# Second feed-forward block of a two-layer trunk: up projection as seven block products, down projection in five chunks

## The chip, the cores and the metric

One core of a Trainium2 chip runs the whole program. The metric is the device time of one execution in microseconds (us). The engines meant below are TensorE (PE, its weight loads shown apart as PEld), VectorE (DVE), ScalarE (ACT), GpSimd (POOL) and SyncE (SP, which here only issues transfers). Each takes its instructions strictly in the order of its own queue.

## The reference

One inference step of a two-layer trunk on 640 tokens of width 1024: 512 tokens of a 64-wide grid and 128 context tokens. Each layer is attention (latent attention in the first, neighbourhood and windowed attention in the second), then a feed-forward block. What the change concerns is the feed-forward block of the second layer:

```
h = modulate(rmsnorm(x), shift, scale)                 # 640 tokens x 1024
u = h @ w_up                                           # 1024 -> 2 * 2816: sides a and g
u = depthwise convolution of 3 taps along the tokens   # zero ends for each group of tokens
x = x + gate * ((u_a * silu(u_g)) @ w_down)            # 2816 -> 1024
y = rmsnorm(x)                                         # behind the second layer
```

All inputs and results are float32.

## The kernel before

Activations lie feature-major: 128 features on the partitions, the tokens along the row. A row has 642 columns: 512 tokens, a zero column, 128 tokens, a zero column; it is processed in two halves, `HALF = ((0, 352), (352, 642))`. A float32 matrix product is made of three passes with float32r operands: each operand is split into a high part (a cast on ACT, line 115) and a low part, the operand less its high part (a subtraction on DVE or POOL, line 111). One product of a 128x128 weight tile with a half of the tokens is so three matmuls: high by high, high by low, low by high (line 135).

The feed-forward block, `ffn_body`, runs over 22 tiles f of 128 inner features, and over two sides for each (a and g). For one f and side, `load_w` brings 512 KB of weights on the SP queue into a tile `raw` of a ring of three, splits them into `whi` and `wlo` (rings of three each), and 48 matmuls go into a two-bank PSUM tile `mm` (8 tiles of 128 input features, 3 passes, 2 halves). `evac` reads that PSUM tile: one ACT activation (middle tap and bias, line 499), two `scalar_tensor_tensor` on DVE (the other taps, lines 500 and 502). When both sides are there: silu on ACT (508), a product on DVE (509), and the split of the result into `g` (cast on ACT, subtraction on DVE).

After 8 tiles f (then 8, then 6) the down projection of these tiles runs over 8 output tiles j, and `add_x` (line 442) adds each result to the residual stream `x` from PSUM. In the last chunk it runs over one half of the tokens and then the other, with the squares for the last norm behind it (line 399 adds them, on POOL or DVE), and a tail that scales and stores the result (line 1525).

In front of the block, `out_proj` makes the attention's output projection half by half; the norm of a half of the tokens (lines 354 to 376, then 419, 432, 433) runs while PE makes the next thing. For the second half PE starts with the first halves of the first three up products (`lead(jobs, h, 3)`): 72 matmuls.

The order of the work in this block is not written out by hand: the program is recorded, and a scheduler lays each engine's queue in order; each instruction then waits, at its place in its queue, for what it needs.

Of the kernel before, what the change touches and what calls it, by code (L numbers as in the profile page):

```python
# [35 lines left out]
HA = 352  # L36
# [6 lines left out]
# The orders in which the steps of a phase are issued; a token names a step, its numbers and, at the end, another engine than Pool  # L43
# for the part of it that may move (d: DVE, a: ACT).
# The steps of mla_in.
# [14 lines left out]
# The units of the attention behind it, two for a head.  # L60
# [6 lines left out]
# The heads of the odd layer, two of a pair after one another.  # L67
# [20 lines left out]
class Trunk:  # L88
# [9 lines left out]
    # ---------------------------------------------------------------- helpers  # L98
# [14 lines left out]
    def split(self, hi, lo, src, lo_engine=None):  # L113
        """Two float32r parts whose sum is src."""
        self.nc.scalar.copy(hi, src)  # L115
        self.low(lo, src, hi, lo_engine)
# [22 lines left out]
    def proj_steps(self, ps, w, rhs, half, stride=P, off=0, m=P, order=None):  # L139
        """Half of the tokens of a feature-major product: (w columns off..off+m of each k tile)^T times rhs."""  # L140
# [14 lines left out]
    def proj_late(self, w, rhs):  # L155
        """A product whose last k tile is left to the function returned."""
# [20 lines left out]
    def acts(self):  # L177
        """A new set of activations [half][k] -> (hi, lo); halves in slots of their own."""
        return [[None] * KT, [None] * KT]

    def act(self, half):
        w = HALF[half][1] - HALF[half][0]
        return tuple(self.T(self.hp, "h" + "ab"[half], [P, w], F32R, 16) for _ in range(2))

    # ----------------------------------------------------- queue of PE filling
# [20 lines left out]
    def after(self, a, b):  # L206
        """Issue a after b, on their common engine."""
# [84 lines left out]
    def mod_step(self, mode):  # L292
        """One k tile of a piece of a modulation vector; mode "d": without the other engines, "i": products in place."""
# [32 lines left out]
    def mod_finish(self, ps_tag, age=0):  # L326
        """The sums over partitions of the vectors whose sums over k tiles were issued a while ago."""
# [1361 lines left out]
```

## Time and profile before

| what | value |
|---|---|
| median of 3 runs | 1730.47 us (1729.17 to 1732.49) |
| profiled execution, first to last instruction (span) | 1726.0 us |
| mean granted TensorE clock | 0.975 |
| PE busy | 1611.3 us, 93% of the span |
| DVE, ACT, POOL busy | 1156.3, 862.9, 594.2 us |

The profile shows one execution; the medians of the runs lie 4.5 us above its span. Rows of groups give line, engine, operation, output tile <- input tiles, shape and count, then total busy time, the mean of one in nanoseconds, and the idle time before. Rows in order of time begin with the start and the length in us; "x3" marks instructions that were merged. Rows of stretches give, after the stretch and its length, the busy time of PE, PEld, DVE, ACT and POOL with their numbers of instructions, the granted clock, the DMA share and GB/s.

### The profile page before, as it was taken

Reading aid. Unit: us, or ns where it says so; the run is one execution under the profiler, and the core shown is the slowest. Engines: PE = TensorE matmul, PEld = TensorE weight load, DVE = VectorE, ACT = ScalarE, POOL = GpSimd, SP = SyncE. Lnnn points to the kernel's source line nnn. Section 1 sums busy time; section 2 is a strip of 40 time slices with the busy share of each in tenths; the row PEclk is TensorE's granted clock in tenths of the full one; section 3 lists DMA queues with packets and bytes.
Section 4 is the critical chain, followed back from the end, with each engine's and each line's share of the span. In section 5 each row is a group of like instructions: output and inputs, shape, how many; then the busy total and the mean of one; then the engine's idle time right before and its main releaser. Section 6 shows DMA issues by size and latency. Waiting matters only on the chain.

```text
span 1726.0 us, 27729 instructions
## 1 busy us (share of the span) xinstructions
PE 1611.3 (93%) x10565; PEld 1542.0 (89%) x10565; DVE 1156.3 (67%) x1901; ACT 862.9 (50%) x1570; POOL 594.2 (34%) x565
## 2 busy tenths in 40 slices
PE   8877888888999999999998999989999999999996
PEld 2777877788899999999998999978999999999996
DVE  4895888768888779977548677763755435543536
ACT  3545767644555345543345678784443213321344
POOL 2164667563253433443063344665100000000044
PEclk9988999989999999999999999998999999999998
DMA  9431221063344444444235111132122222222223
GB/s 337 136 103 51 62 67 63 13 204 104 104 159 142 147 141 154 149 149 131 67 109 174 56 51 52 56 102 89 38 86 74 74 74 75 75 80 77 68 74 116
DMA packets 74850, 176.11 MB, mean 102 GB/s; under 512 B 11134, under 2 KB 22734, under 8 KB 74718
## 3 DMA queue, kind: packets, MB, share of 16 engines
q1 hardware_dynamic: 72222, 170.08, 30.8%
q10 hardware_dynamic: 2304, 4.20, 0.7%
q8 instruction: 83, 1.36, 0.3%
q14 instruction: 49, 0.40, 0.1%
q0 software_dynamic: 192, 0.07, 0.0%
HBM read 167.24 MB, written 8.03 MB: 102 GB/s over the span
## 4 chain that ended last, share of the span: by engine, by line
PE 61%; DVE 11%; ACT 4%; issue 3%; DMA 3%; POOL 1%; DVEq 0%; SPq 0%; ACTq 0%; POOLq 0%
PE mm L135 55%; DMA mraw<-in_w_mod_dram 2%; DVE wlo L111 1%; DVE acc L311 1%; PE sc L1196 1%; PE o L1246 1%; PE tr L1234 1%; DVE nt L419 1%; POOL wlo L111 1%; DVE u L500 1%; ACT whi L115 1%; DVE pt L111 0%; DMA raw<-in_w_out_dram 0%; PE b L354 0%; DVE ha L433 0%
## 5 line engine op out<-in xcount | busy, mean ns | idle before, releaser
L135 PE MATMUL mm<-ha,whi 128*128 128x352 f32 (+1 forms) x1920 | 472.1, 328 | 11.5 <-ACT ha L432 4.6
L135 PE MATMUL mm<-hb,whi 128*128 128x290 f32 (+1 forms) x1920 | 398.3, 300 | 2.6 <-ACT hb L432 1.3
L135 PEld LDWEIGHTS mm<-ha,whi 128*128 128x128 f32 (+1 forms) x1920 | 334.6, 190 | 14.6 <-ACT ha L432 4.7
L115 ACT CAST whi<-raw 128x1024 fp32r<-128x1024 f32 (+2 forms) x194 | 192.9, 999 | 306.6 <-PE mm L135 282.4
L111 POOL TENSOR_TENSOR wlo<-raw,whi 128x768 fp32r<-128x768 f32 (+3 forms) x60 | 125.6, 2099 | 618.9 <-ACT whi L115 551.1
L135 PE MATMUL mm<-g,whi 128*128 128x352 f32 (+1 forms) x1408 | 315.6, 312 | 7.5 <-DVE x L442 7.1
L135 PEld LDWEIGHTS mm<-hb,whi 128*128 128x128 f32 (+1 forms) x1920 | 317.1, 191 | 5.4 <-issue 2.5
L135 PE MATMUL mm<-ha,wlo 128*128 128x352 f32 (+1 forms) x960 | 312.3, 325 | 0.0
L135 PE MATMUL mm<-hb,wlo 128*128 128x290 f32 (+1 forms) x960 | 286.8, 299 | 0.0
L309 POOL TENSOR_TENSOR acc<-acc,mt 128x512 f32<-128x512 f32 x115 | 178.9, 1556 | 258.1 <-ACT mt L308 255.3
L111 DVE TENSOR_TENSOR wlo<-raw,whi 128x1024 fp32r<-128x1024 f32 (+1 forms) x134 | 172.1, 1287 | 117.1 <-ACT whi L115 116.4
L135 PEld LDWEIGHTS mm<-g,whi 128*128 128x128 f32 x1408 | 238.8, 191 | 9.4 <-issue 4.0
L135 PE MATMUL mm<-g,wlo 128*128 128x352 f32 (+1 forms) x704 | 220.2, 313 | 2.4 <-POOL wlo L111 1.6
L311 DVE SCALAR_TENSOR_TENSOR acc<-mraw,cs,acc 128x512 f32<-128x512 f32 (+1 forms) x165 | 163.7, 999 | 49.5 <-DMA mraw<-in_w_mod_dram 47.7
L135 PEld LDWEIGHTS mm<-hb,wlo 128*128 128x128 f32 (+1 forms) x960 | 183.5, 191 | 0.4 <-issue 0.2
L135 PEld LDWEIGHTS mm<-ha,wlo 128*128 128x128 f32 (+1 forms) x960 | 181.6, 189 | 0.5
L442 DVE SCALAR_TENSOR_TENSOR x<-mm,mod,x 128x128 f32<-128x128 f32 (+3 forms) x160 | 71.4, 477 | 129.2 <-PE mm L135 129.2
L308 ACT ACTIVATE mt<-mraw,cs 128x512 f32<-128x512 f32 x115 | 81.8, 720 | 113.3 <-DMA mraw<-in_w_mod_dram 99.0
L135 PEld LDWEIGHTS mm<-g,wlo 128*128 128x128 f32 x704 | 134.0, 190 | 3.4 <-POOL wlo L111 2.2
L500 DVE SCALAR_TENSOR_TENSOR u<-mm,convw,u 128x641 f32<-128x641 f32 x88 | 77.4, 879 | 22.4 <-ACT u L499 22.4
L819 POOL TENSOR_TENSOR p<-p,s 128x640 f32<-128x640 f32 x48 | 63.5, 1343 | 61.2 <-DVE s L812 57.9
L502 DVE SCALAR_TENSOR_TENSOR u<-mm,convw,u 128x641 f32<-128x641 f32 x88 | 77.7, 883 | 2.2
(248 smaller groups left out, 2533.9 us busy)
## 6 DMA issues: line engine op xcount, KB each, us to landing
raw<-in_w_up_dram SPq DMA_DIRECT2D x88, 512.0 KB, 3.4
mraw<-in_w_mod_dram SPq DMA_DIRECT2D x128, 256.0 KB, 2.9
raw<-in_w_down_dram SPq DMA_DIRECT2D x32, 512.0 KB, 3.5
raw<-in_w_down_dram SPq DMA_DIRECT2D x32, 384.0 KB, 3.1
raw<-in_w_in_odd_dram SPq DMA_DIRECT2D x18, 512.0 KB, 3.6
mraw<-in_w_mod_dram SPq DMA_DIRECT2D x16, 512.0 KB, 8.7
raw<-in_w_out_dram SPq DMA_DIRECT2D x16, 512.0 KB, 3.9
x<-in_xT_dram SPq DMA_DIRECT2D x16, 321.0 KB, 6.0
```

Source lines behind the costliest of these rows:

```text
L111: (engine or self.nc.vector).tensor_sub(lo, src, Fv(hi))
L115: self.nc.scalar.copy(hi, src)
L135: self.pe = self.nc.tensor.matmul(out, lhsT=l, rhs=r, start=k == 0, stop=k == n - 1)
L308: nc.scalar.activation(t, raw, AF.Copy, scale=s)
L309: nc.gpsimd.tensor_add(acc, acc, t)
L311: nc.vector.scalar_tensor_tensor(out=acc, in0=raw, scalar=s, in1=acc, op0=ALU.mult, op1=ALU.add)
L419: self.nc.vector.scalar_tensor_tensor(out=t[:, c], in0=x[k][:, c0:c1][:, c], scalar=self.mod[l][:, ma, k, v : v + 1], in1=rs[:, c], op0=AL ...
L442: nc.vector.scalar_tensor_tensor(out=xt[:, a:b], in0=ps[:, a:b], scalar=self.mod[l][:, m, j, v : v + 1], in1=xt[:, a:b], op0=ALU.mult, op1 ...
L500: nc.vector.scalar_tensor_tensor(out=u[:, 1:W], in0=ps[:, 0 : W - 1], scalar=cw[:, j, 0:1], in1=u[:, 1:W], op0=ALU.mult, op1=ALU.add)
L502: nc.vector.scalar_tensor_tensor(out=u[:, 0 : W - 1], in0=ps[:, 1:W], scalar=cw[:, j, 2:3], in1=u[:, 0 : W - 1], op0=ALU.mult, op1=ALU.add)
L819: nc.gpsimd.tensor_tensor(out=p_, in0=p_, in1=u.s[:, j : j + 1].to_broadcast(list(p_.shape)), op=ALU.mult)
L1196: nc.tensor.matmul(ps[:, c : c + n], lhsT=u.Q[:, a], rhs=x[e], start=e == 0, stop=e == 1)
```

## The change

The two halves of the tokens are made equal, 322 and 320 columns, in the whole program (`HA = 322`). For the second layer's feed-forward block a class `Mix` takes the place of `ffn`.

For one f the product has two sides of the output, two halves of the 1024 input features and two halves of the tokens: eight block products of 12 matmuls. With the weight blocks A11, A12 (side a, lower and upper input features) and A21, A22 (side g), and the activation blocks B11, B12, B21, B22 (input features by half of the tokens), they are replaced by seven products (Strassen's identity in Winograd's form): A11 B11, A12 B21, and five products of sums of blocks (T1 to T4 and B22 name their right-hand operands). `norm` makes the sums of the activation blocks once, behind the norm of the second half of the tokens. `mixed` makes four sums of weight blocks for every f, on POOL (lines 1643 to 1647 of the changed kernel), and splits the results: `sp` (1024 wide, low part on DVE), `gp` (1024 wide, in `whi`/`wlo`, low part on POOL) and `s4p` (512 wide, low part on POOL). `up` combines the seven results with two ACT copies (L1628, L1633) and five DVE additions (L1659, L1666, L1667, L1669, L1672), each of a PSUM and an SBUF operand, into two SBUF tiles `u`; `conv` then works on these instead of on PSUM (L1683 to L1689). The first three f begin ahead with A11 B11 and A12 B21 (`LEAD`). The down projection runs in five chunks of 5, 5, 4, 4 and 4 tiles f, each after the up projection of one tile more, and now into one-bank PSUM tiles by half of the tokens. The ring `raw` keeps its three tiles, and now holds both sides' weights of an f until `mixed` is done with them.

```diff
-HA = 352
+HA = 322
...
@@ run
-            with self.psums(wide), self.pool("ffn1") as pool:
...
-                x, h = self.out_proj(pool, 1, oT, xd, lambda: None)
...
+                    x, _ = self.out_proj(pool, 1, oT, xd, lambda: None, mix=mix)
...
-                self.ffn(pool, 1, h, x, lambda n: None, tail)
...
+                    mix.ffn(pool, pi, x, lambda: None, tail)
+class Mix:
...
+    LEAD = 3
+    CHUNKS = ((0, 5), (5, 10), (10, 14), (14, 18), (18, 22))
+    PSUMS = {"p": (1, 6), "b": (1, 2)}
...
+    def norm(self, pool, wpool, x, acc, half):
...
+        for q in range(n):
+            a, b = self.first.pop(q), self.pair()
...
+            for j in range(2):
+                self.shifted(b[:, j], x, rs, 1, q + j * n)
...
+            nc.vector.tensor_sub(a[:, 0], b[:, 0], a[:, 0])
+            nc.gpsimd.tensor_sub(c, b[:, 1], b[:, 0])
+            nc.vector.tensor_sub(b[:, 0], b[:, 1], a[:, 0])
+            nc.vector.tensor_sub(a[:, 1], a[:, 1], b[:, 0])
+            self.rows["T2", q] = self.parts([h[:, 0] for h in ht], b[:, 0], nc.vector)
+            self.rows["T1", q] = self.parts(t.wide_act(1), a[:, 0], nc.vector)
+            self.rows["T3", q] = self.parts([h[:, 1] for h in ht], c, nc.gpsimd)
+            self.rows["B22", q] = self.parts(t.wide_act(1), b[:, 1], nc.vector)
+            self.rows["T4", q] = self.parts([h[:, 2] for h in ht], a[:, 1], nc.gpsimd)
...
+    def begin(self, f):
...
+        st["raw"] = ra, _ = [t.raw(t.i["w_up"][self.l, f, side], D) for side in range(2)]
+        st["A"] = tuple(self.T(t.wp, tag, [P, D], F32R, 3) for tag in ("whi", "wlo"))
+        t.split(*st["A"], ra, nc.vector)
+        st["c"] = self.pair(), self.pair()
+        st["p"] = t.PS("p")
+        self.product(st["p"], st["A"], 0, "B11")
+        nc.scalar.copy(st["c"][1][:, 0], st["p"][:, 0:HA])
...
+    def begun(self, st):
+        self.product(st["p"], st["A"], self.B, "B21", False)
+        self.nc.scalar.copy(st["c"][0][:, 0], st["p"][:, 0:HA])
+    def mixed(self, st):
...
+        ra, rg = st["raw"]
+        s = self.T(pi, "s", [P, 2 * n], F32, 1)
+        s4 = self.T(pi, "s4", [P, n], F32, 1)
+        sp, s4p = ([self.T(pi, f"{tag}{e}", [P, m], F32R, 1) for e in "hl"] for tag, m in (("sp", 2 * n), ("s4p", n)))
+        gp = [self.T(t.wp, tag, [P, D], F32R, 3) for tag in ("whi", "wlo")]
+        nc.gpsimd.tensor_add(s[:, 0:n], rg[:, 0:n], rg[:, n:])
+        nc.gpsimd.tensor_sub(s[:, n:], s[:, 0:n], ra[:, 0:n])
+        t.split(*sp, s, nc.vector)
+        nc.gpsimd.tensor_sub(rg[:, 0:n], ra[:, 0:n], rg[:, 0:n])
+        nc.gpsimd.tensor_sub(s4, ra[:, n:], s[:, n:])
+        t.split(*gp, rg, nc.gpsimd)
+        t.split(*s4p, s4, nc.gpsimd)
...
+    def up(self, f, st, early):
...
+        sp, gp, s4p = self.mixed(st)
...
+        self.product(ps, sp, n, "T2")
+        nc.vector.tensor_add(ca[:, 1], ps[:, 0:HA], cg[:, 0])
+        if not early:
+            self.begun(st)
...
+        self.product(pd, sp, 0, "T1")
...
+        self.product(ps, gp, 0, "T3")
+        nc.vector.tensor_add(cg[:, 0], ps[:, 0:HA], ca[:, 1])
+        nc.vector.tensor_add(cg[:, 1], pd[:, 0:HA], cg[:, 0])
+        self.product(pd, s4p, 0, "B22", False)
+        nc.vector.tensor_add(ca[:, 1], pd[:, 0:HA], ca[:, 1])
...
+        self.product(ps, gp, n, "T4")
+        nc.vector.tensor_add(cg[:, 0], ps[:, 0:HA], cg[:, 0])
...
+        for f0, f1 in self.CHUNKS:
+            for f in range(f0, min(f1 + 1, NFF)):
+                if f not in g:
+                    up(f)
...
+                for j in range(KT):
+                    w = load(j, nc.gpsimd if j % 2 else nc.vector)
+                    for half in range(2):
+                        ps = t.PS("p")
+                        self.down(ps, w, g, fs, half, True)
+                        self.add(j, x[j], ps, half)
```

Three places of the queues matter for what follows; buffer numbers tell the tiles of one f from those of the next.

POOL between the last norm and the block. Before, POOL only clears columns there and then has nothing until the end:

```order
L399 TENSOR_TENSOR sq_2618_13687<-sq_2616_13657,sq_2618_13687 128x290
L428 MEMSET hb_13763 128x2
L429 MEMSET hb_13764 128x2
```

Now (`nt`, `ht`: the last of the activation sums and its low parts; raw_13903 and raw_13905: the two sides' weights of f = 0, raw_13940 and raw_13942: of f = 1):

```order
L1598 TENSOR_TENSOR nt_13876<-u_13863 128x322
L111 TENSOR_TENSOR ht_13875<-nt_13876,ht_13874 128x322
L111 TENSOR_TENSOR ht_13875<-first_13487,ht_13874 128x322
L1643 TENSOR_TENSOR s_14014<-raw_13905 128x512
L1644 TENSOR_TENSOR s_14014<-s_14014,raw_13903 128x512
L1646 TENSOR_TENSOR raw_13905<-raw_13903,raw_13905 128x512
L1647 TENSOR_TENSOR s_2677_14015<-raw_13903,s_14014 128x512
L111 TENSOR_TENSOR s4pl_14019<-s_2677_14015,s4ph_14018 128x512
L1643 TENSOR_TENSOR s_14117<-raw_13942 128x512
L1644 TENSOR_TENSOR s_14117<-s_14117,raw_13940 128x512
L1646 TENSOR_TENSOR raw_13942<-raw_13940,raw_13942 128x512
L1647 TENSOR_TENSOR s_2693_14118<-raw_13940,s_14117 128x512
```

The weight sums of f = 0 and f = 1 stand behind the whole of the norm's work on POOL. With three tiles `raw`, the g side of f = 1 is loaded into the tile that raw_13903 leaves (after L1647 of f = 0), and the a side of f = 2 into the tile that raw_13940 leaves (after L1647 of f = 1).

PE at the same place (p_13950: f = 1, p_13987: f = 2; whi_13981: the a side of f = 2; sph_14016: the first mixed weights of f = 0). Before, three up products on the first half of the tokens, `ha`, followed one another here:

```order
L1615 MATMUL p_13950<-ha_13514,whi_13944 128x322
L1615 MATMUL p_13950<-ha_13515,whi_13944 128x322
L1615 MATMUL p_13950<-ha_13514,wlo_13945 128x322
L1615 MATMUL p_13987<-ha_13469,whi_13981 128x322
L1615 MATMUL p_13987<-ha_13470,whi_13981 128x322
L1615 MATMUL p_14032<-ht_13778,sph_14016 128x322
L1615 MATMUL p_14032<-ht_13779,sph_14016 128x322
L1615 MATMUL p_13987<-ha_13469,wlo_13982 128x322
```

The first matmul of f = 2 stands behind the 48 of f = 0 and f = 1 and ahead of everything that uses the second half of the tokens.

DVE for one f in the middle of a chunk, before (mm: PSUM):

```order
L111 TENSOR_TENSOR wlo_14162<-raw_14159,whi_14161 128x1024
L509 TENSOR_TENSOR u_13969<-u_13969,u_13997 128x642
L500 SCALAR_TENSOR_TENSOR u_14031<-mm_13914,convw,u_14031 128x641
L111 TENSOR_TENSOR g_14004<-u_13969,g_14003 128x642
L502 SCALAR_TENSOR_TENSOR u_14031<-mm_13914,convw,u_14031 128x641
L111 TENSOR_TENSOR wlo_14227<-raw_14224,whi_14226 128x1024
L500 SCALAR_TENSOR_TENSOR u_14090<-mm_14041,convw,u_14090 128x641
L502 SCALAR_TENSOR_TENSOR u_14090<-mm_14041,convw,u_14090 128x641
```

and now (p: PSUM; the taps L1684 and L1685, of which a fourth stands just ahead, belong to f = 2, the additions to f = 3, spl_14490 to f = 4, wlo_14608 to f = 5):

```order
L1684 SCALAR_TENSOR_TENSOR u_14313<-u_13986,convw,u_14313 128x641
L1685 SCALAR_TENSOR_TENSOR u_14308<-u_13985,convw,u_14308 128x641
L1685 SCALAR_TENSOR_TENSOR u_14313<-u_13986,convw,u_14313 128x641
L1659 TENSOR_TENSOR u_14331<-p_14365,u_14332 128x322
L111 TENSOR_TENSOR spl_14490<-s_14487,sph_14489 128x1024
L1689 TENSOR_TENSOR u_14308<-u_14308,u_14313 128x642
L1666 TENSOR_TENSOR u_14332<-p_14405,u_14331 128x322
L1667 TENSOR_TENSOR u_14332<-p_14392,u_14332 128x322
L111 TENSOR_TENSOR g_14320<-u_14308,g_14319 128x642
L1672 TENSOR_TENSOR u_14332<-p_14433,u_14332 128x322
L1681 MEMSET u_14332 128x2
L111 TENSOR_TENSOR wlo_14608<-raw_14603,whi_14607 128x1024
```

The four taps read SBUF on both sides where they read PSUM before, and five additions from PSUM are new; on POOL, which was empty here, six instructions now stand for every f (L1643, L1644, L1646, L1647 and two low parts). The matmuls of B22, PE's second product into the tile that L1667 reads, wait for L1667.

More of the change, by code (lines that the diff above doesn't have):

```diff
@@ L182, in act, with wide_act @@
         w = HALF[half][1] - HALF[half][0]
-        return tuple(self.T(self.hp, "h" + "ab"[half], [P, w], F32R, 16) for _ in range(2))
+        return tuple(t[:, 0:w] for t in self.wide_act(half))
+    def wide_act(self, half):
+        return tuple(self.T(self.hp, "h" + "ab"[half], [P, HA], F32R, 16) for _ in range(2))
     def add_job(self, key, gen):
@@ L443, in add_x, with out_proj @@
                                                in1=xt[:, a:b], op0=ALU.mult, op1=ALU.add)
-    def out_proj(self, pool, l, oT, xsrc, after, early=()):
+    def out_proj(self, pool, l, oT, xsrc, after, early=(), mix=None):
         nc = self.nc
@@ L465, in out_proj @@
                 self.mod_finish("b")
-                self.norm_half(pool, h, x, acc, half, l, 3, 4)
+                if mix:
+                    mix.norm(pool, wpool, x, acc, half)
+                else:
+                    self.norm_half(pool, h, x, acc, half, l, 3, 4)
         return x, h
@@ L723, in put_act, with raw, fetch @@
             self.split(*oT[half][k], src[:, a:b], lo_engine)
-    def fetch(self, src, n, pool=None, tags=("whi", "wlo"), bufs=3):
+    def raw(self, src, n):
         raw = self.T(self.wp, "raw", [P, n], F32, 3)
         self.nc.sync.dma_start(raw, src)
+        return raw
+    def fetch(self, src, n, pool=None, tags=("whi", "wlo"), bufs=3):
+        raw = self.raw(src, n)
         def parts(lo_engine=self.nc.gpsimd):
@@ L1515, in run @@
                 self.odd(pool, nh, oT, bias_full, (wide, odd))
-            with self.psums(wide), self.pool("ffn1") as pool:
-                self.mods_in(pool, len(self.todo), 2, nc.sync)
-                x, h = self.out_proj(pool, 1, oT, xd, lambda: None)
+            with self.pool("ffn1") as pool, self.pool("ffn1_mix") as pm:
+                mix = Mix(self, 1, pm)
+                with self.psums(wide):
+                    x, _ = self.out_proj(pool, 1, oT, xd, lambda: None, mix=mix)
                 def tail(half, acc):
@@ L1523, in tail @@
                     for k in range(KT):
-                        y = self.T(pool, "y", [P, HA], F32, 8)[:, 0 : b - a]
-                        (nc.gpsimd if k in (1, 4, 6) else nc.vector).tensor_mul(y, x[k][:, a:b], rs)
-                        nc.sync.dma_start(o["y"][:, k, a:b], y)
-                self.ffn(pool, 1, h, x, lambda n: None, tail)
+                        if k % 2 == 0:
+                            y = mix.pair()
+                        (nc.gpsimd if k in (1, 4, 6) else nc.vector).tensor_mul(y[:, k % 2, 0 : b - a], x[k][:, a:b], rs)
@@ L1667 @@
     from concourse.bass_utils import run_bass_kernel_spmd as _run
-    nc = _bacc.Bacc("TRN2", target_bir_lowering=False, num_devices=1)
+    nc = _bacc.Bacc("TRN2", target_bir_lowering=False, num_devices=1, dynamic_dma_scratch_size=4096)
     arrays, ins, outs = {}, {}, {}
```

124 lines of the change are left out of this document (added).

## The prediction

> **What bounds the kernel now.** I read the page's busy times and slices first, then stretches around the block (columns as in the section on the profile above; the number in brackets counts instructions).
>
> ```profile
> PE 1611.3 (93%) x10565; PEld 1542.0 (89%) x10565; DVE 1156.3 (67%) x1901; ACT 862.9 (50%) x1570; POOL 594.2 (34%) x565
> PE   8877888888999999999998999989999999999996
> POOL 2164667563253433443063344665100000000044
> ...
> 1235.20:1247.60 12.40, 12.40 (x75) 11.97 (x74) 9.88 (x32) 6.59 (x17) 0.00 (x0) 1.00 0.01 2
> ...
> 1250.00:1660.00 410.00, 410.00 (x2774) 410.00 (x2773) 191.97 (x217) 127.43 (x145) 3.71 (x2) 1.00 0.23 74
> ...
> 1650.00:1700.00 50.00, 47.60 (x312) 46.55 (x311) 23.53 (x31) 27.57 (x43) 28.85 (x20) 1.00 0.35 101
> ...
> 1700.00:1710.00 10.00, 7.28 (x43) 6.83 (x43) 8.93 (x17) 4.16 (x10) 4.96 (x4) 0.83 0.44 157
> ...
> 1710.00:1726.00 16.00, 5.24 (x33) 4.21 (x31) 7.13 (x14) 3.39 (x7) 3.01 (x3) 0.75 0.22 74
> ```
>
> PE is busy for all of 410 us in the second layer's block, DVE for 192, ACT for 127, POOL for 4. So the block costs what PE's matmuls cost, and every other engine has room: this is the favourable ground for doing fewer matmuls and more additions. Just ahead, while the norm of the second half of the tokens runs (1235 to 1247), PE is busy too, since the first halves of three up products are there to be done. Only the last 76 us lose PE time, 2.4 + 2.7 + 10.8 = 15.9 us.
>
> **Term 1, fewer matmuls.** 410.00 / 2774 = 0.1478 us from one matmul to the next, at a mean of 321 columns. Up projection before: 22 x 96 = 2112 matmuls, 312.2 us. Now 22 x 7 x 12 = 1848, of 322 columns; costing the extra column at its share, 0.1483: 274.0. **-38.2 us.** The down projection keeps its 1056 matmuls and its mean width. Elsewhere the equal halves move columns from one product to another: 0, give or take 2.
>
> **Term 2, the opening.** Here a stall arises where there is none. The durations:
>
> ```profile
> 1234.47 0.65 DVE L442 SCALAR_TENSOR_TENSOR x<-mm,mod,x 128x160 f32<-128x160 f32 x2 [2.58 <-PE mm L135]
> ...
> 1238.86 0.46 DVE L376 TENSOR_TENSOR r<-r,r 128x290 f32<-128x290 f32 x1
> ...
> L419 DVE SCALAR_TENSOR_TENSOR nt<-x,mod,r 128x160 f32<-128x160 f32 x2 | 0.8, 382 | 0.0
> ...
> L419 DVE SCALAR_TENSOR_TENSOR nt<-x,mod,r 128x128 f32<-128x128 f32 x1 | 0.3, 349 | 0.0
> ...
> L399 DVE TENSOR_TENSOR sq<-sq,sq 128x352 f32<-128x352 f32 x2 | 1.1, 525 | 1.3 <-ACT sq L397 1.3
> ...
> L111 POOL TENSOR_TENSOR q<-q,q 128x352 fp32r<-128x352 f32 x10 | 9.4, 941 | 3.2 <-ACT q L115 3.2
> ...
> L111 POOL TENSOR_TENSOR hb<-o,hb 128x290 fp32r<-128x290 f32 x9 | 7.3, 806 | 0.0
> ...
> L998 POOL TENSOR_TENSOR z<-z,z 128x512 f32<-128x512 f32 x3 | 3.9, 1300 | 0.2
> ...
> raw<-in_w_up_dram SPq DMA_DIRECT2D x88, 512.0 KB, 3.4
> ...
> L115 ACT CAST whi<-raw 128x1024 fp32r<-128x1024 f32 x57 | 59.6, 1049 | 210.9 <-PE mm L135 210.9
> ```
>
> And how DVE and POOL stand to one another, in order of time (start, length):
>
> ```profile
> 911.72 4.19 POOL L111 TENSOR_TENSOR wlo<-raw,whi 128x768 fp32r<-128x768 f32 x2
> ...
> 912.07 0.38 DVE L442 SCALAR_TENSOR_TENSOR x<-mm,mod,x 128x160 f32<-128x160 f32 x1
> ...
> 912.36 1.85 DVE L433 SCALAR_TENSOR_TENSOR ha<-nt,mod,ha 128x352 fp32r<-128x352 f32 x1
> ...
> 914.40 1.89 DVE L433 SCALAR_TENSOR_TENSOR ha<-nt,mod,ha 128x352 fp32r<-128x352 f32 x1
> ...
> 1216.59 0.58 DVE L433 SCALAR_TENSOR_TENSOR ha<-nt,mod,ha 128x352 fp32r<-128x352 f32 x1
> ...
> 1217.08 1.22 DVE L111 TENSOR_TENSOR wlo<-raw,whi 128x1024 fp32r<-128x1024 f32 x1
> ...
> 1217.42 1.56 POOL L399 TENSOR_TENSOR sq<-sq,sq 128x290 f32<-128x290 f32 x1 [15.14 <-ACT sq L397]
> ...
> 1218.22 1.14 DVE L433 SCALAR_TENSOR_TENSOR ha<-nt,mod,ha 128x352 fp32r<-128x352 f32 x1
> ```
>
> A DVE instruction with two SBUF inputs that takes 0.58 alone takes 1.85 and 1.89 beside a POOL instruction, one that reads PSUM keeps its 0.38, and POOL's own is drawn out too. They take turns. From 1217.08 to 1219.36 are 2.28 us, and the three lengths alone are 1.22 + 0.81 + 0.58 = 2.61: a POOL instruction between two of DVE saves 0.33 against their sum, no more.
>
> Now the chain, from the end of the last output product (0 is 1234.5). The norm's factor is there at 1239.32, so 4.8. Then DVE has 16 scalings (8 x 0.35, and 8 of 190 columns, 0.44 by the rows of 128 and 160: 6.3) and 24 subtractions of 322 columns (0.49, between 0.461 and 0.525: 11.8), POOL 12 (0.87, between 0.806 and 0.941: 10.4), each needing what DVE and ACT made just before. In turns: 6.3 + 11.8 + 10.4 - 12 x 0.33 = 24.5, so POOL is free at 29.3. Only then come its four weight sums of f = 0 (4 x 1.30 = 5.2): 34.5. They free the tile of `raw` that the second load of f = 1 needs: 3.4, 37.9. The sums of f = 1: 43.1. They free the tile for f = 2: 46.5. Its cast: 47.6. PE has 48 matmuls of f = 0 and f = 1 until there, 7.1 us, and its queue then stands at the first of f = 2, with all mixed products behind it; on SP every later weight load stands behind the one that waits, so nothing else can be fetched around it. **+41 us** (47.6 - 7.1 = 40.5, and the norm's own sums, which stood behind up products before, come first). Lower bound, if DVE and POOL ran side by side and successive DVE instructions overlapped by 0.08: 33. Upper, with no 0.33 saved (+4) and the clock as low after the pause as the 0.75 of the last row above: 48.
>
> **Term 3, DVE and POOL in turns for every f.**
>
> ```profile
> L111 POOL TENSOR_TENSOR wlo<-raw,whi 128x1024 fp32r<-128x1024 f32 x26 | 64.6, 2486 | 86.7 <-ACT whi L115 58.4 <-PE sc L1196 19.7 <-DMA kh<-kh 8.6
> ...
> L111 POOL TENSOR_TENSOR wlo<-raw,whi 128x512 fp32r<-128x512 f32 x3 | 3.8, 1274 | 27.1 <-ACT whi L115 27.1
> ...
> L111 DVE TENSOR_TENSOR wlo<-raw,whi 128x1024 fp32r<-128x1024 f32 x57 | 69.7, 1225 | 106.4 <-ACT whi L115 106.4
> ...
> L500 DVE SCALAR_TENSOR_TENSOR u<-mm,convw,u 128x641 f32<-128x641 f32 x43 | 37.9, 880 | 6.7 <-ACT u L499 6.7
> ...
> L111 DVE TENSOR_TENSOR g<-u,g 128x642 fp32r<-128x642 f32 x21 | 17.4, 828 | 15.9 <-ACT g L115 15.9
> ...
> L509 DVE TENSOR_TENSOR u<-u,u 128x642 f32<-128x642 f32 x21 | 17.4, 828 | 18.2 <-ACT u L508 18.2
> ...
> L442 DVE SCALAR_TENSOR_TENSOR x<-mm,mod,x 128x352 f32<-128x352 f32 x3 | 1.7, 583 | 8.7 <-PE mm L135 8.7
> ...
> L508 ACT ACTIVATE u<-u 128x642 f32<-128x642 f32 x21 | 15.6, 742 | 45.3 <-DVE u L502 45.3
> ```
>
> PE needs 84 x 0.1483 = 12.5 us for one f. POOL gets 4 x 1.30 + 2.49 + 1.27 = 9.0. DVE gets, with two SBUF inputs, two low parts (2.45), four taps (3.52; they read PSUM before), the product (0.83) and g's low part (0.83): 7.6; and five additions from PSUM (0.55 each by the row of 352 columns at 583: 2.8), which fall under POOL's turns. Each engine alone stays below 12.5. Taking turns with a saving of 0.33 at each of POOL's six, they need 7.6 + 9.0 - 2.0 = 14.6, 2.1 more than PE. The queues tie them together: spl of f + 1 is one buffer and waits for T1 of f, POOL's next sums wait for spl, and PE's B22 waits for L1667, behind the taps on DVE. So nothing runs ahead by more than one f, and a DVE or POOL that is late comes back to PE as a pause. In the first run of six f, f = 1 and 2 have only 60 matmuls left (8.9 us): 2 x 5.7 + 3 x 2.1 = **+17**. Later runs have 5, 4, 4 and 3 f; the first two of each I take as prepared during the down projection, where POOL and DVE have little: 8 x 2.1 = **+17**. Bounds: 3 (no turns: DVE's 10.4 against 8.9, twice) and 60 (nothing saved, 16.6 for an f: 2 x 7.7 + 11 x 4.1).
>
> [...]
>
> **Term 4, the end.** The last g now needs, behind the last product, an activation (0.89, as long as a tap), four taps (3.5), silu (0.74), product, cast and low part (2.4): 7.5, 8.5 with handovers, and 30 matmuls (4.4) to cover it. In the last run an output tile has 12 matmuls, 1.78, against POOL's 1.27 + 0.87 for weights and squares: 0.37 for each of eight. 4 + 3 - 1 for the wait that goes from 1650 to 1700: **+6** (-3, if the narrower tiles end sooner, to +12).
>
> **Sum** against the profiled 1726.0: -38 + 41 + 17 + 17 + 6 = +43, a span of 1769. The median lies 4.5 us above the span: **1773 us**. Edits at nothing: the two ACT copies and casts (ACT had 127 of 410), more loads of `w_down` in smaller pieces (DMA share 0.23).
>
> **Rivals.** B, *the turns are hidden*: PSUM tiles (six) and two buffers let PE run past what DVE is late with, so that only the opening remains: -38 + 41 + 0 + 3 + 3 = +9, about 1740. For it: DVE and POOL fill 14.6 us only if their work collides all the time. Against: B22's wait has no other product between. C, *DVE and POOL do not exclude one another here*: opening 33, later 3, end 3: -38 + 33 + 3 + 3 = +1, 1731, not slower; it decides once the opening falls under 30. For it: 0.38 shows that some pairs run together. Against: 1.85 and 1.89. D, *nothing is saved at a change of turn*: -38 + 45 + 60 + 6 = +73, 1803. For it: the first pair at 911.72 ends at 914.21 where 1.86 + 0.58 in a row end at 914.16. E, *the block is one gain*: the loads of f = 1 and 2 come before the sums, so that the opening costs 5: -38 + 5 + 17 + 17 + 6 = +7, or -27 with C too. Against it: the ring of three and the two orders shown above.
>
> **How the numbers follow.** The forecast 0.56 (alone 1752 to 1790); B 0.20; C 0.10; D 0.10; E 0.04. Leaving 1 in 10 above and below, the range is 1735 to 1806. A measurement of this kernel tells 0.2%, 3.5 us, from no change. Faster: two thirds of C and some of E, 0.09; within: 0.04, the rest of C and the low edge of B; slower: 0.87.
>
> **What would show it.** Right: about 40 us without PE at the place of 1235, released by the cast (L115) of an up weight, this by its load, this by L1647; then PE pauses of about 2 us for L1667 once an f; taps and POOL subtractions drawn out against 0.88 and 1.30. Wrong: PE at 0.9 or more in the first 50 us of the block, or an f that repeats every 12.5 us, or a matmul pitch other than 0.148.

## The result and the profile after

The changed kernel takes 1802.01 us (median of 4 runs, 1800.71 to 1804.05) beside 1731.48 for the kernel before, measured with it: a ratio of 1.0413, 95% interval 1.0397 to 1.0429, 70 us slower. The profiled execution has a span of 1798.9 us, 72.9 more than that of before. The forecast was 1773, slower, with a range of 1735 to 1806.

The page of the changed kernel, busy times and slices of the span:

```profile
PE 1605.7 (89%) x10301; PEld 1522.8 (85%) x10301; DVE 1283.1 (71%) x2127; ACT 925.3 (51%) x1702; POOL 833.6 (46%) x717
PE   8868888889999999999979999888379989898986
POOL 2174777462333243331542346752563754546434
```

PE has 264 matmuls fewer, as the change says, and yet is busy only 6 us less: many matmuls of the block run at about half pace (0.27 us in place of 0.148), of which more below, and ahead of the block PE is busy 7 us more (1142 for 1135). The slice with a 3 is the opening of the block; behind it come slices of 8 where a row of nines stood. What PE waited for from 1200 us on (line waited for, total us, times, longest):

```profile
PE p L1615 <- DVE u L1667: 27.3, 20, 3.2
PE p L1615 <- ACT whi L115: 26.4, 1, 26.4
PE p L1615 <- ACT u L1628: 8.0, 5, 5.5
PE p L1615 <- DVE spl L111: 7.7, 2, 4.9
PE p L1700 <- ACT g L115: 3.5, 1, 3.5
PE p L1700 <- DVE wlo L111: 3.0, 1, 3.0
```

The one wait of 26.4 us and the twenty for L1667 are those that the prediction named. Of the 8.0 us for the copy L1628, 7.1 lie in the opening, ahead of the long wait. To see where all of it went I took, from the trace, the time from the start of each matmul to that of the next, less 0.148 us, and summed it by stretch. This counts pauses and slow matmuls alike. The first column is the end of the last output product, where the block begins.

```
us beyond 0.148 per matmul   block begins   opening and first run   later runs   last down products, end
before                          1234.3             1.4                 0.2               8.8
changed                         1244.2            59.9                34.2              16.8
```

The change thus reads: 264 x 0.148 = -39.1, opening and first run +58.5, later runs +34.0, end +8.0, and 9.9 ahead of the block; +71.3 of the 72.9. Of the rest 0.9 lies behind the last matmul.

**The opening**, in order of time, POOL, ACT and PE of the changed kernel:

```profile
1270.27 0.75 POOL L111 TENSOR_TENSOR ht<-first,ht 128x322 fp32r<-128x322 f32 x1 [1.33 <-ACT ht L115]
1270.98 1.26 POOL L1643 TENSOR_TENSOR s<-raw 128x512 f32<-128x512 f32 x1
...
1280.82 1.26 POOL L1643 TENSOR_TENSOR s<-raw 128x512 f32<-128x512 f32 x1 [1.79 <-DMA raw<-in_w_up_dram]
...
1284.60 1.26 POOL L1647 TENSOR_TENSOR s<-raw,s 128x512 f32<-128x512 f32 x1
...
1273.62 1.05 ACT L115 CAST sph<-s 128x1024 fp32r<-128x1024 f32 x1 [3.42 <-POOL s L1644]
...
1289.56 2.94 ACT L115 CAST whi<-raw 128x1024 fp32r<-128x1024 f32 x3 [11.86 <-DMA raw<-in_w_up_dram]
...
1290.65 0.91 PE L1615 MATMUL p<-ha,whi 128*128 128x322 f32 x2 [26.41 <-ACT whi L115]
```

The norm's last instruction on POOL, then the sums of f = 0, then a wait for a load, the sums of f = 1, another load, the cast, and PE goes on. The first mixed weights of f = 0 had been ready at 1274.7 (sph), 16 us before, behind the matmul of f = 2 in PE's queue.

**A later f.** Groups of DVE and POOL from 1415 to 1486 us, and the product L1689 of two f that follow one another:

```profile
L1684 DVE SCALAR_TENSOR_TENSOR u<-u,convw,u 128x641 f32<-128x641 f32 x8 | 12.1, 1553 | 3.2 <-ACT u L1683 3.2
L1685 DVE SCALAR_TENSOR_TENSOR u<-u,convw,u 128x641 f32<-128x641 f32 x8 | 6.7, 878 | 0.0
L1689 DVE TENSOR_TENSOR u<-u,u 128x642 f32<-128x642 f32 x4 | 7.9, 1973 | 2.2 <-ACT u L1688 2.2
L111 POOL TENSOR_TENSOR wlo<-raw,whi 128x1024 fp32r<-128x1024 f32 x5 | 14.1, 2819 | 5.3 <-ACT whi L115 5.3
```

```profile
1437.40 2.08 DVE L1689 TENSOR_TENSOR u<-u,u 128x642 f32<-128x642 f32 x1 [0.47 <-ACT u L1688]
1452.32 2.08 DVE L1689 TENSOR_TENSOR u<-u,u 128x642 f32<-128x642 f32 x1 [0.47 <-ACT u L1688]
```

The first tap of each side (L1684) takes 1.55 where a tap took 0.88; the second (L1685) keeps its 0.88. The product takes 1.97 in place of 0.83, POOL's low part 2.82 in place of 2.49. In the middle of this run an f repeats every 14.92 us, where PE needs 12.5.

### The profile page after: what moved, and what is told of

It is laid out like the page before. It is cut to its first block, busy times and chain, and to the rows that moved or that the text cites. A ratio compares the mean times of both kernels' runs of the same rounds, so it can differ in the third digit from the quotient of the medians.

```text
span 1798.9 us, 27888 instructions
## 1 busy us (share of the span) xinstructions
PE 1605.7 (89%) x10301; PEld 1522.8 (85%) x10301; DVE 1283.1 (71%) x2127; ACT 925.3 (51%) x1702; POOL 833.6 (46%) x717
## 4 chain that ended last, share of the span: by engine, by line
PE 49%; DVE 27%; ACT 8%; issue 6%; DMA 5%; POOL 4%; SPq 0%; DVEq 0%; ACTq 0%; POOLq 0%
PE mm L135 28%; PE p L1700 7%; PE p L1615 6%; DMA mraw<-in_w_mod_dram 3%; DVE acc L314 3%; DVE u L1684 2%; DVE wlo L111 2%; DVE nt L422 1%; PE tr L135 1%; DVE u L1689 1%; DVE g L111 1%; DVE nm L807 1%; PE o L1256 1%; PE tr L1244 1%; PE sc L1206 1%
## 5 line engine op out<-in xcount | busy, mean ns | idle before, releaser
L111 POOL TENSOR_TENSOR wlo<-raw,whi 128x1024 fp32r<-128x1024 f32 (+4 forms) x98 | 200.2, 2047 | 328.5 <-ACT whi L115 287.5
L115 ACT CAST whi<-raw 128x1024 fp32r<-128x1024 f32 (+3 forms) x210 | 193.7, 929 | 218.8 <-PE mm L135 49.1
L135 PE MATMUL mm<-ha,whi 128*128 128x322 f32 (+1 forms) x1216 | 282.0, 319 | 8.3 <-ACT ha L435 4.7
L135 PE MATMUL mm<-hb,whi 128*128 128x320 f32 (+1 forms) x1216 | 277.5, 316 | 0.7 <-ACT hb L435 0.6
L135 PEld LDWEIGHTS mm<-ha,whi 128*128 128x128 f32 (+1 forms) x1216 | 208.5, 193 | 10.6 <-ACT ha L435 4.8
L314 DVE SCALAR_TENSOR_TENSOR acc<-mraw,cs,acc 128x512 f32<-128x512 f32 (+1 forms) x165 | 174.4, 1064 | 49.9 <-DMA mraw<-in_w_mod_dram 48.5
L135 PE MATMUL mm<-ha,wlo 128*128 128x322 f32 (+1 forms) x608 | 192.5, 317 | 0.0
L135 PE MATMUL mm<-hb,wlo 128*128 128x320 f32 (+1 forms) x608 | 190.9, 314 | 0.0
L111 DVE TENSOR_TENSOR wlo<-raw,whi 128x1024 fp32r<-128x1024 f32 (+2 forms) x112 | 147.1, 1314 | 41.7 <-ACT whi L115 37.2
L135 PE MATMUL mm<-g,whi 128*128 128x322 f32 (+1 forms) x704 | 159.2, 313 | 5.3 <-ACT ha L435 3.7
L1700 PE MATMUL p<-g,whi 128*128 128x322 f32 (+1 forms) x704 | 159.9, 315 | 4.2 <-ACT g L115 3.5
L1700 PEld LDWEIGHTS p<-g,whi 128*128 128x128 f32 x704 | 121.0, 192 | 5.1 <-ACT g L115 3.7
L1615 PE MATMUL p<-ha,whi 128*128 128x322 f32 x352 | 85.4, 330 | 34.4 <-ACT whi L115 26.4
L1700 PE MATMUL p<-g,wlo 128*128 128x322 f32 (+1 forms) x352 | 111.0, 316 | 3.9 <-DVE wlo L111 3.0
```

The costliest lines, as they stand in the source:

```text
L111: (engine or self.nc.vector).tensor_sub(lo, src, Fv(hi))
L135: self.pe = self.nc.tensor.matmul(out, lhsT=l, rhs=r, start=k == 0, stop=k == n - 1)
L314: nc.vector.scalar_tensor_tensor(out=acc, in0=raw, scalar=s, in1=acc, op0=ALU.mult, op1=ALU.add)
L1615: self.t.pe = self.nc.tensor.matmul(ps[:, 0:HA], lhsT=l_, rhs=r, start=fresh and n == 0, stop=n == 3 * self.KP - 1, skip_group_check=True)
L1700: self.t.pe = self.nc.tensor.matmul(ps[:, 0 : b - a], lhsT=l_[:, k * P : (k + 1) * P], rhs=r, start=first and n == 0, stop=last and n == 3 ...
```

## The experiments

The theory: POOL's queue and the ring of `raw` hold the opening; later, DVE and POOL take turns, so that an f lasts longer than its matmuls. The rivals stand with each run. Sums "beyond 0.148" are those of the table above, for the kernel of the run. What is changed is always told against the changed kernel, but for the first run.

### The equal halves alone

```diff
-HA = 352
+HA = 322
```

> The kernel before with the halves of the tokens made 322 and 320 columns and nothing else changed. In the changed kernel the last output product of the second layer ended 9.9 us later than before, ahead of everything else that was changed. Theory: this comes from the equal halves alone; then this kernel takes 1740 to 1743 us, with the block itself as long as before (491 us from the last output product to the end). Rival: it comes from the rest of the change (other pools, other PSUM tiles); then it takes 1730 to 1733.

1739.02 us beside 1731.08: ratio 1.0048, interval 1.0030 to 1.0066, so 5 to 11 us. The norm's sums behind the last output product, before and in this kernel:

```profile
1234.27 1.14 PE L354 MATMUL b<-sq,ones 128*128 128x290 f32 x4
```

```profile
1241.71 1.24 PE L354 MATMUL b<-sq,ones 128*128 128x320 f32 x4
```

From there to the end it is 491.7 us before and 492.4 here. The halves cost their 8 us ahead of the block and nothing in it, as the theory had it, though the time lies 1 us under its 1740. A single execution tells this only roughly: in kernels whose work ahead of the block is the same, these sums began at 1244.2, 1246.7, 1241.9 and 1247.2.

### Two f begun ahead in place of three

```diff
-    LEAD = 3
+    LEAD = 2
```

> The changed kernel with two f begun ahead in place of three (LEAD = 2), so that the first product of f = 2 no longer stands ahead of the mixed products. Theory (the ring of raw and POOL's queue hold the opening): PE goes on when the sums of f = 0 are split, some 12 us earlier than with three, and then waits some 3 us more for f = 1: 1790 to 1795. Rival (the norm's own sums hold it, whatever stands in front): with 24 matmuls fewer to fill the wait the time stays at 1802 or rises by up to 4.

1787.34 us (ratio to before 1.0336, interval 1.0309 to 1.0363), 15 less than the changed kernel. The rows that end PE's longest wait of the block here and the first one behind it:

```profile
1273.62 0.91 PE L1615 MATMUL p<-ht,sph 128*128 128x322 f32 x2 [10.62 <-ACT sph L115]
...
1285.51 0.56 PE L1615 MATMUL p<-ht,sph 128*128 128x322 f32 x2 [1.70 <-ACT sph L115]
```

PE now goes on with the mixed weights as soon as they are split, 31 us after the last output product in place of 46, and waits 1.7 and 2.1 us again for those of f = 1. Opening and first run lose 47.7 us in place of 59.9. Less work ahead was better, since what stood ahead was itself waiting. That is the theory's way; the gain is 3 us more than its range gave.

### The norm's sums on DVE

```diff
-            nc.gpsimd.tensor_sub(c, b[:, 1], b[:, 0])
+            nc.vector.tensor_sub(c, b[:, 1], b[:, 0])
...
-            self.rows["T3", q] = self.parts([h[:, 1] for h in ht], c, nc.gpsimd)
+            self.rows["T3", q] = self.parts([h[:, 1] for h in ht], c, nc.vector)
...
-            self.rows["T4", q] = self.parts([h[:, 2] for h in ht], a[:, 1], nc.gpsimd)
+            self.rows["T4", q] = self.parts([h[:, 2] for h in ht], a[:, 1], nc.vector)
```

> The changed kernel with the norm's twelve POOL instructions (T3's difference, the low parts of T3 and T4) on DVE, nothing else. POOL then makes the sums of f = 0 some 24 us earlier, but those of f = 1 wait for the low part of f = 0 on DVE, which stands behind the norm. Theory (ring and queues): the first matmul of f = 2 comes at 40 in place of 46 us after the last output product: 4 to 8 us less than the changed kernel, 1794 to 1798. Rival (POOL's place behind the norm is all): 12 to 20 us less.

1793.14 us in a single run, 9 less; the long wait of PE:

```profile
1282.60 0.90 PE L1615 MATMUL p<-ha,whi 128*128 128x322 f32 x2 [18.34 <-ACT whi L115]
```

It falls by 8.1 us, nearer to the theory's 4 to 8 than to 12 to 20: POOL's place behind the norm was only a part. What held POOL in its stead:

```profile
1271.16 1.78 POOL L111 TENSOR_TENSOR s4pl<-s,s4ph 128x512 fp32r<-128x512 f32 x1 [25.49 <-ACT s4ph L115]
```

POOL has the sums of f = 0 done at once, and then waits with the low part of s4p for a cast that stands on ACT behind those of the norm; the sums of f = 1 come behind it.

### POOL reads nothing

Memsets of the same length for POOL's six instructions of an f, for instance:

```diff
-        nc.gpsimd.tensor_add(s[:, 0:n], rg[:, 0:n], rg[:, n:])
-        nc.gpsimd.tensor_sub(s[:, n:], s[:, 0:n], ra[:, 0:n])
+        nc.gpsimd.memset(s, 0.5)
+        nc.gpsimd.memset(s[:, 0:300], 0.5)
+        nc.gpsimd.memset(s, 0.25)
+        nc.gpsimd.memset(s[:, 0:300], 0.5)
```

> The changed kernel with the four weight sums and the two low parts that POOL makes for every f replaced by POOL memsets of about the same length (each 1.30 us sum by memsets of 1024 and some 300 columns, the low parts by memsets of 2.5 and 1.25 us), which write the same tiles and read nothing: the mixing of the weights is left out. The norm's POOL work stays. Theory (DVE and POOL take turns): the taps fall from 1.55 us to 0.88 and the waits for L1667 from 27 us to under 6, the time to 1755 to 1768. Rival (L1667 is late by its place in DVE's queue, behind instructions that wait for ACT): the waits for L1667 stay above 15 us, the time at 1790 or more.

1740.62 us in a single run, 61 less. A run in the middle: busy times by engine, DVE's first taps (L1695 here), product (L1700) and one of POOL's memsets:

```profile
1384.00:1444.00 60.00, 60.00 (x401) 59.36 (x401) 40.33 (x64) 31.97 (x45) 34.90 (x59) 1.00 0.22 67
```

```profile
L1695 DVE SCALAR_TENSOR_TENSOR u<-u,convw,u 128x641 f32<-128x641 f32 x8 | 6.8, 886 | 3.2 <-ACT u L1694 3.2
L1700 DVE TENSOR_TENSOR u<-u,u 128x642 f32<-128x642 f32 x4 | 4.2, 1038 | 4.6 <-ACT u L1699 4.6
L1643 POOL MEMSET s<- 128x1024 f32 x4 | 3.8, 954 | 4.0 <-DVE spl L111 4.0
```

With POOL nearly as busy (34.90 of 60 us, where it had 44.39 of 71 in the changed kernel), the tap is back at 0.886 and PE hardly pauses; the one wait for L1667 (L1678 here) takes 0.4 us. Of the four products three take 0.83 and one, which meets a low part that POOL makes for the down projection, 1.67. The later runs lose 4.0 us in place of 34.2. So the 34 us hang on POOL's reading instructions; neither POOL's time nor DVE's order alone makes them. That they work through the turns is seen in the lengths of tap and product. How much of the gain came in another way this run doesn't tell: a memset of s does not wait for the load that the sum would read, and one of a low part not for its cast. The whole gained more than expected, since the opening shrank as well (59.9 to 26.4 with the first run); for the opening this run is no clean test.

### Side g in PSUM

```diff
-    PSUMS = {"p": (1, 6), "b": (1, 2)}
+    PSUMS = {"p": (1, 5), "b": (1, 1), "c": (2, 1)}
...
-        nc.vector.tensor_add(cg[:, 1], pd[:, 0:HA], cg[:, 0])
+        cc = t.PS("c")[:, 512 - HA : 512 + HA]
+        nc.vector.tensor_add(cc[:, HA:], pd[:, 0:HA], cg[:, 0])
```

> The changed kernel with the side g that L1667 and L1672 make written to a two-bank PSUM tile instead of SBUF (five product tiles and one for sums in place of six and two), so that two of the four taps have one SBUF input only. Everything is computed. Theory (turns): 1.76 us for every f leave the turns, the cycle falls from 14.6 to some 12.9 us, the 34 us that the later runs lose fall under 12: 1772 to 1782. Rival (latency of the chain, not turns): 1798 to 1806, since no instruction was taken out of the chain and a product tile is missing.

1798.52 us (ratio 1.0392, interval 1.0365 to 1.0420): only 3.5 less, outside what the theory gave. The groups from 1412 to 1480 us (L1690 is the product):

```profile
L1690 DVE TENSOR_TENSOR u<-u,u 128x642 f32<-128x642 f32 x4 | 9.1, 2283 | 3.7 <-ACT u L1689 3.7
...
L1685 DVE SCALAR_TENSOR_TENSOR u<-u,convw,u 128x641 f32<-128x641 f32 x4 | 4.7, 1168 | 3.2 <-ACT u L1684 3.2
...
L1685 DVE SCALAR_TENSOR_TENSOR u<-c,convw,u 128x641 f32<-128x641 f32 x4 | 3.5, 873 | 0.0
```

The taps that read PSUM are free of POOL (0.87 us), as the theory had it. But the product, still on SBUF, now meets POOL's longest instruction and takes 2.28 in place of 1.97, and DVE waits longer for silu. In the middle of a run an f repeats every 13.9 us, 1 us less, and yet the later runs lose 32.9. Their start got worse: from the first matmul of B22 of the first f to that of the second went 16.3, 16.3, 18.1 and 18.8 us in the four runs, where it was 15.3, 16.9, 15.3 and 16.1. Summing the lengths that exclude one another was too simple: it also matters which instructions meet, and the order that the scheduler laid out didn't avoid it.

### The whole convolution through PSUM

```diff
-    PSUMS = {"p": (1, 6), "b": (1, 2)}
+    PSUMS = {"p": (1, 4), "c": (2, 2)}
...
-            v = self.pair().rearrange("p j c -> p (j c)")
+            v = self.pair().rearrange("p j c -> p (j c)") if side else t.PS("c")[:, 512 - HA : 512 + HA]
...
-        nc.vector.tensor_mul(u[0], u[0], u[1])
+        nc.vector.tensor_mul(cc, u[0], u[1])
```

> The changed kernel with both sides of the convolution kept so that no tap, product or low part of g has two SBUF inputs: side g and its product with silu lie in a two-bank PSUM tile, the tapped side a in another; four product tiles in place of six. DVE keeps 2.45 us with two SBUF inputs for an f in place of 7.6, the instructions and their order are otherwise the same, and everything is computed. Theory (turns): with POOL's 9.0 that makes 11.4, under PE's 12.5, so the later runs lose under 10 us in place of 34 and the first under 10 in place of 17: 1762 to 1778. Rival (after e5, which gained 3.5 us where 20 to 30 were expected: the handovers between DVE and ACT in a fixed order set the cycle, turns or not): 1790 to 1800.

1775.03 us (ratio 1.0247, interval 1.0216 to 1.0278), 27 less. The low part of the mixed weights and the product, 1403 to 1469 us:

```profile
L112 DVE TENSOR_TENSOR spl<-s,sph 128x1024 fp32r<-128x1024 f32 x4 | 8.3, 2075 | 7.3 <-ACT sph L116 7.3
...
L1692 DVE TENSOR_TENSOR c<-c,u 128x642 f32<-128x642 f32 x4 | 3.3, 830 | 2.1 <-ACT u L1691 2.0
```

Everything that reads PSUM has the length it had in the kernel before (taps 0.88 us, product 0.83); the two low parts of weights from SBUF take what turns are left (2.08 and 1.51 for 1.22). The later runs lose 18.3 in place of 34.2, where the theory gave under 10. With nothing left out of the computation, half of the loss is traced to the turns of the convolution; the rest may lie with POOL against the two low parts, tried last.

### The opening made anew

On top of the last kernel; the norm by products, and loads of their own for the f begun ahead, which are four in place of three. The main parts:

```diff
+        for q, (a, b, ht) in enumerate(bs):
+            c = self.T(pool, "nt", [P, HA], F32, 2)
+            nc.vector.tensor_sub(a[:, 0], b[:, 0], a[:, 0])
+            nc.vector.tensor_sub(c, b[:, 1], a[:, 0])
+            nc.vector.tensor_sub(a[:, 1], a[:, 1], c)
+            self.rows["T2", q] = self.parts([h[:, 0] for h in ht], c, nc.vector)
...
+        if f < self.LEAD:
+            ra = t.raw(t.i["w_up"][self.l, f, 0], D)
...
+        if "raw" not in st:
+            st["raw"] = [t.raw(t.i["w_up"][self.l, st["f"], side], D) for side in range(2)]
```

> e6 with the opening made anew: the sums of activations and their low parts are all on DVE and in the order in which the products need them (T2, T1, T4, then T3 and B22 behind the sums of f = 0), so that POOL makes the weight sums of f = 0 at once; the four f begun ahead load side a alone and load it again for the sums, so that no load of raw waits for a sum. The same computation, 4 loads more. Theory (the opening is held by POOL's queue and the ring of raw): the 41 us become 15 to 22, 18 to 26 us less than e6. Rival (the norm's chain on DVE, 29 us, holds the opening whatever POOL does): 0 to 10 us less than e6.

1765.40 us (ratio 1.0197, interval 1.0166 to 1.0228), 10 less than the last: the upper edge of the rival, half of the theory. PE's waits in the opening and after:

```profile
1259.49 0.75 PE L1626 MATMUL p<-ha,whi 128*128 128x322 f32 x2 [4.58 <-ACT u L1643]
...
1276.62 0.81 PE L1626 MATMUL p<-ht,sph 128*128 128x322 f32 x2 [5.03 <-ACT sph L116]
...
1325.07 0.90 PE L1626 MATMUL p<-hb,s4ph 128*128 128x322 f32 x2 [3.25 <-DVE c L1687]
```

The stall of 26 us is gone: two of 5 us are left (the first because a copy on ACT stands behind the norm's activations). But opening and first run together fall only from 49.7 to 37.3. An f begun ahead has 60 matmuls left, 8.9 us, but from the first matmul of B22 of f = 0 to that of f = 1 went 18.8 us, and 16.3 to that of f = 2, so that much of what the opening gave came back as pauses within the first run. Several things were changed at once here, so the gain is not divided among them.

### The old halves ahead of the block

```diff
+set_halves(352)
+MIX_HALF = ((0, 322), (322, W))
...
+            set_halves(322)
             with self.pool("ffn1") as pool, self.pool("ffn1_mix") as pm:
```

> e7 with the halves of 352 and 290 columns everywhere but from the second layer's output projection on, where they are 322 and 320. Theory (the equal halves cost 8 to 10 us ahead of the block, by e1): 6 to 10 us less than e7. Rival (they cost it in the second layer's output projection and norm): no difference. If e6 and e7 come out by their theories this is 1730 to 1746, beside 1731 before.

1757.18 us (ratio 1.0140, interval 1.0110 to 1.0170), 8.2 less: the 8 us of the equal halves again, from the other side.

### Down products between the up products

```diff
-    CHUNKS = ((0, 5), (5, 10), (10, 14), (14, 18), (18, 22))
+    CHUNKS = ((0, 2), (2, 4), (4, 7), (7, 10), (10, 13), (13, 16), (16, 19), (19, 22))
...
+                more = range(*self.CHUNKS[i + 1])
+                for q, f in enumerate(more):
+                    up(f)
+                    self.f0 = f0
+                    for j in range(q * KT // len(more), (q + 1) * KT // len(more)):
```

> e8 with the down projection cut in eight runs of 2, 2 and then 3 f, and its products put between the up products of the next run (2 or 3 output tiles behind each f) in place of behind the whole run; the same computation, with 8 additions to each x in place of 5. Theory (for an f DVE and POOL need 13 us, PE 12.5 and with the leads 8.9, so PE waits in the up stretches and DVE and POOL idle in the down stretches): PE has some 19 us of work for an f now, DVE some 17; the 19 us of the later runs nearly vanish and the 36 us of opening and first run become 20 to 26: 1722 to 1738. Rival (each instruction waits in a fixed order, so the additions to x, which wait for PE, hold up what PE waits for): 1750 to 1775.

> The same with runs of 3, 3, 3, 3, 3, 3, 2 and 2 f, so that the first down products come one f later. Theory: the stall of the first f lasts longer, 2 to 6 us more than with a first run of two, and the end is 1 to 3 us dearer or cheaper. Rival: no difference between the two.

1839.38 and 1832.88 us (ratios 1.0616 and 1.0584, both within 0.003), 82 and 76 more than the kernel they were built on, and worse than the rival's figure. The second was expected at 2 to 6 us more than the first, or the same, and took 6.5 less, which stays unexplained. From the first, PE's waits over the block, and one of POOL's from 1500 to 1600 us:

```profile
PE p L1729 <- DVE x L1738: 37.6, 22, 5.3
PE p L1634 <- DVE x L1738: 21.9, 10, 4.1
```

```profile
POOL s L1668 <- DMA raw<-in_w_up_dram: 14.8, 2, 11.2
```

PE waits for the additions to x (L1738), which empty the four product tiles, and POOL for loads into the ring of three `raw`, which the weights of both projections now pass through by turns. Every engine has room on average (from 1500 to 1600 us PE is busy for 86.3, DVE for 53.4, ACT for 35.0, POOL for 44.8), and each waits for another in turn. It was the rival's mechanism, at a higher price.

### POOL's low parts to DVE

On the kernel of 1757 us, first the one line, then both:

```diff
-        t.split(*gp, rg, nc.gpsimd)
-        t.split(*s4p, s4, nc.gpsimd)
+        t.split(*gp, rg, nc.vector)
+        t.split(*s4p, s4, nc.vector)
```

> e8 with the low part of gp, POOL's longest instruction (2.49 us), made by DVE (1.23 us). Theory (turns): for an f the instructions that exclude one another fall from 2.45 + 9.0 to 3.7 + 6.5 us and DVE's own work rises from 10.1 to 11.3, still under 12.5: the later runs lose 8 to 14 us in place of 19, 1745 to 1754. Rival (what is left of the waits is DVE's own queue, not POOL): 2 to 12 us more than e8, 1759 to 1769.

> The same with the low part of s4p on DVE too, so that POOL makes the four sums only: 4.3 + 5.2 us exclude one another, DVE's own work is 11.9. Theory (turns): as e10 or up to 4 us less. Rival (DVE's queue): another 2 to 8 us more than e10.

1747.31 us (ratio 1.0104, interval 1.0074 to 1.0134), then 1743.70 (1.0082, 1.0058 to 1.0106). A run of the second, and what PE still waited for there:

```profile
1383.00:1440.00 57.00, 56.70 (x380) 56.18 (x379) 48.47 (x71) 30.68 (x42) 24.13 (x17) 1.00 0.26 74
```

```profile
PE p L1634 <- DVE c L1695: 9.1, 7, 3.0
```

DVE is given more work, at 48.5 of 57 us, and PE pauses less: the later runs lose 7.7 and 9.7 us in place of 18.6. Fewer turns were worth more than DVE's time. The step from the first to the second, 3.6 us, lies within the intervals, and the later runs have no part in it. All the same, in the second opening and first run still lose 32.6 us and the end 16.7, as much as in the changed kernel, and no version came below the kernel before.

## Why the prediction came out as it did

The sign and most of the mechanism held; the time came out 29 us above the forecast, and above the 1752 to 1790 that the forecast was given by itself. That it lies in the range is luck: the range's upper part was there for rival D, which is not what happened. Of the 29 us, 17 belong to the later runs and some 8 to what lies ahead of the block.

**Term 1, fewer matmuls: right.** 264 x 0.148 = 39; where PE was not held it kept its pace, 60.00 us for 401 matmuls with POOL reading nothing, 0.150 each for 0.148.

**Term 2, the opening, +41: right, step by step.** POOL was free of the norm 26.8 us after the last output product (29.3 forecast), the load for f = 1 was used at 36.6 (37.9), the sums of f = 1 were done at 41.7 (43.1), PE went on at 46.5 (47.6). 46.5 - 7.1 = 39.4. (A scaling of 190 columns, read as 0.44, takes 0.41 in the run with the norm on DVE, a quarter of a microsecond in all.)

**Term 3, first run, +17: right.** 58.5 - 39.4 leaves 19 for it. From the first matmul of B22 of one f to that of the next went 16.0 and 15.2 us where 8.9 were to be done, then 15.2, 15.6 and 12.5 for 12.5: 7.1 + 6.3 + 2.7 + 3.1, also 19 (forecast 5.7 twice and 2.1 three times).

**Term 3, later runs, +17: half of what it was, and this is the larger miss.** The cycle in the middle of a run was nearly right (14.92 for 14.6). The step that failed is "the first two of each I take as prepared during the down projection". PE waited for L1667 before every one of the 16 f, from 1380 us on:

```profile
PE p L1615 <- DVE u L1667: 22.6, 16, 3.2
```

The first two f of the four runs, put at nothing, have 15.1 us of this, and the other eight 7.5. What held the first f, rows of DVE and PE at the start of the second run:

```profile
1423.80 2.25 DVE L111 TENSOR_TENSOR spl<-s,sph 128x1024 fp32r<-128x1024 f32 x1 [4.28 <-ACT sph L115]
1425.97 0.48 DVE L1666 TENSOR_TENSOR u<-p,u 128x322 f32<-128x322 f32 x1
1426.49 0.49 DVE L1667 TENSOR_TENSOR u<-p,u 128x322 f32<-128x322 f32 x1
...
1427.04 0.57 PE L1615 MATMUL p<-hb,s4ph 128*128 128x322 f32 x2 [1.13 <-DVE u L1667]
```

This f was itself prepared, but its L1667 stands on DVE behind spl of the next f, and so waits for the next f's sums. In each of the four runs DVE was idle for 3.9 to 6.0 us ahead of that spl, which then took 2.2 us in place of 1.22, beside a low part of POOL. The split of the sums has one buffer, so it can't be made earlier than T1 of the f before. The prediction had that, and did not follow it to the first f of a run. The sum 16 x 2.1 = 34 equals the measured 34.2 by chance: the last f of each run waited under 0.7 us, three of the first ones 2.7 to 3.2, and the 34.2 has slow matmuls in it.

**Elsewhere, "0, give or take 2": wrong.** The equal halves cost 8 us ahead of the block (5 to 11), shown twice. I had counted columns, which are the same in sum. It is not waits alone: up to the block PE is busy for 1142.2 us in the changed kernel and 1135.5 before. What makes it so is left open.

**Term 4, the end, +6: nearly right,** 8.0.

**The rivals.** 1802 is nearly rival D's 1803, but not by D's way: without any saving an f would have lasted 16.6 us, and it lasted 14.92. B (the turns are hidden) and C (none) fell with the 34 us and with the memsets. E fell with the wait of 26.4 us. What was drawn out beside POOL were DVE's instructions with two SBUF inputs: the first tap of a side took 1.55 us on average in the changed kernel, and with side g in PSUM taps with two SBUF inputs took 1.17 and 1.22 and those with one 0.87. The sum of the lengths, 16.6, is 1.7 too high here.

## What to carry to other kernels

Before moving work to an idle engine, ask whose instructions it draws out: here POOL was idle, and giving it 9 us for an f made DVE, which also had room, late for PE (the first tap of a side took 1.55 us in place of 0.88). With POOL's low parts on DVE (1757.18 to 1743.70 us), or with operands kept in PSUM (1802.01 to 1775.03), the kernel was faster. When counting what a stage may prepare in the shadow of another, count the buffers between them, and look at what stands behind the next item's work in an in-order queue: here the result of a prepared f did. And what is put ahead in an in-order queue to fill a wait must not itself wait for what it is to hide.

## What the hardware showed besides

A pause can cost more than its length. Behind nine of the ten pauses of over 2 us in the changed kernel's block, at once or up to 2.1 us later, PE's matmuls run at about 0.27 us in place of 0.148 for 3 us or more: here, in order of time, a pause of 3.23 us with the rows behind it, and the stretch of the opening.

```profile
1550.90 0.91 PE L1615 MATMUL p<-hb,s4ph 128*128 128x322 f32 x2 [3.23 <-DVE u L1667]
1551.60 0.47 PE L1615 MATMUL p<-hb,s4pl 128*128 128x322 f32 x1
1551.87 0.74 PE L1615 MATMUL p<-hb,s4ph 128*128 128x322 f32 x2
1552.41 0.47 PE L1615 MATMUL p<-hb,s4pl 128*128 128x322 f32 x1
```

```profile
1244.10:1290.65 46.55, 12.80 (x56) 10.97 (x54) 23.78 (x48) 19.63 (x47) 22.58 (x21) 0.64 0.08 23
```

From 1551.60 to 1552.41 are three matmuls, 0.27 each; twelve of them lose 1.5 us. The last row is the opening: a mean granted clock of 0.64. Added up over the block, matmuls at this pace lose some 20 us in the changed kernel and 2 in the kernel before, a quarter of what the pauses themselves take (80 us). The length of a pause alone does not decide it: one of 2.61 us was followed by ten slow matmuls, and one of 2.81 us by none; no run here tests what does. The prediction had given this a place only in the upper bound of the opening.

Second, POOL's memsets, which write SBUF and read nothing, did not hold up DVE's taps (0.886 beside 0.880 in the kernel before), with POOL busy for 58% of the time.
